# A two-block transformer kernel: TensorE in written order for its first half, head sums on four column groups, VectorE's row steps and weight splits behind each inverse square root

## Chip, core and metric

The kernel runs on one core of one Trainium2 chip, as one launch. The metric is the device time in microseconds (us) from start to end. Engines go by the profile's names: PE (TensorE; PEld is its weight load), DVE (VectorE), ACT (ScalarE), POOL (GpSimd) and SP (SyncE, here a queue of DMAs).

## What is computed

`x` (256 tokens, width 1024, fp32) first goes through two attention layers (layer 0: sliding-window and dilated attention; layer 1: latent attention with rotary keys) and a norm. Then two layers of a second block follow, each with a mixer (differential attention with normed q and k heads, pooling, a convolution, gates) and a mixture of 16,384 experts called PEER. A second stream of 256 context tokens goes through layer 0 of the second block and serves as keys and values in layer 1.

```python
def rms_norm(x, g):
    y = x * lax.rsqrt(jnp.mean(x * x, axis=-1, keepdims=True) + EPS)
    return y * g
def peer_ffn(x, w_q, sub_keys, u_emb, v_emb):   # 8 heads, top 16 each
    s = einsum(x @ w_q, sub_keys); s1, i1 = top_k(s[..., 0, :], 16); s2, i2 = top_k(s[..., 1, :], 16)
    top_s, pos = top_k(s1[:, None] + s2[None, :], 16); eidx = i1 * 128 + i2 at pos
    hid = gelu(einsum('td,thkd->thk', x, u_emb[eidx]))
    return einsum('thk,thkd->td', softmax(top_s) * hid, v_emb[eidx])
```

## The kernel before

Activations lie transposed: 1024 features as 8 chunks of 128 partitions by 256 tokens. A weight matrix comes as chunks of 128 x 1024 numbers (512 KB), loaded by SP's queue for the x stream and by POOL's for the context stream (`WS.load`). To keep precision with the fast matmul type, `WS.split` makes a high part `wa` on ACT (L281) and a low part `wb = wr - wa` on DVE (L282); `mm3` (L409 to L411) then runs three matmuls per 128 rows, 24 per chunk. Chunks marked whole go as native fp32 (`mm1`, L416).

The streams are Python generators that yield a cost after each piece. `par`, `lead` and `along` take turns among them by these costs, so they set the order in which instructions are written. A scheduler with its own clock then reorders the instructions of each engine: a ready one may be put ahead of one that is written earlier. On the chip each engine runs its own list in order.

`rsqrt` (L396 to L403) is a bit trick and three Newton steps, 13 small DVE instructions in a chain. `rms_bcast` squares on ACT (L472), sums over partitions on PE (L474, four 32-column groups), sums per token (L479), calls `rsqrt`, builds a diagonal (`dg`, L498) and broadcasts it with PE (L501). `qkv` (L946) and `attn2` (L1046) sum each head's squares with a matmul that has the 128 x 128 square as its weight and moves 2 columns or 1; after `rsqrt` they transpose the result (`rows_hl`, L905 or L903), split it into `rh` and `rl` (L907, L908) and spread it with `selT` (L966, L967).

PEER for x (`ffn_start`, `topk`, `gbuild`, `peer`): scores and top 16 on DVE; `gbuild` turns the choices into tables G with one-hot products (L1487, L1489 on DVE, L1495 on PE, L1499 on ACT) and stores them; `peer` streams all of U and V, 128 chunks each: `hid(j)` gives chunk j's hidden values, `wgt(j)` multiplies by G (L1551), `vside(j)` adds W times V (L1576 to L1580). The first `npre` hidden chunks run before the main loop, the first `nnat` of them in native fp32; `NPRE` holds both, per layer.

PEER for the context takes each chosen expert's row by indirect DMA (`rows`, L1381): 512 row steps of 128 x 1024 on DVE, half L1392 (dot products), half L1401 (accumulation). They run beside everything from the middle of layer 0's x mixer on, at the rates in `RATE`.

Of the kernel before, what the change touches and what calls it, by code (L numbers as in the profile page):

```python
# [34 lines left out]
NPRE = (16, 20), (20, 28)  # L35
# [16 lines left out]
for _name, _w in (("ident", 128), ("iota", 128), ("perm", 128), ("sel2", 2),  # L52
                  ("ropeC", 256), ("ropeS", 256), ("edge", 64), ("causal", 256),
                  ("iota16", 16), ("starts", 16), ("fold", 32), ("misc", 8)):
    _C[_name] = (_n, _n + _w)
    _n += _w
# [10 lines left out]
def const_tables():  # L67
# [11 lines left out]
    perm = np.zeros((128, 128), np.float32)  # L79
    perm[p ^ 32, p] = 1.0  # L80
    put("perm", perm)
    put("fold", np.concatenate([np.eye(32, dtype=np.float32)] * 4, 0))
    put("sel2", np.stack([p < 64, p >= 64], 1).astype(np.float32))
# [169 lines left out]
class WS:  # L253
# [18 lines left out]
    def split(s, to):  # L272
        nc = s.k.nc
        while s.ns < min(to, s.n):
# [7 lines left out]
            nc.vector.tensor_tensor(b, r, a, op=OP.subtract)  # L282
# [10 lines left out]
class Ker:  # L293
    def __init__(s, nc, tc, es, ai, ao):
# [6 lines left out]
        s.bufs = dict(BUFS)  # L301
        s.cn = 0
# [91 lines left out]
    def rsqrt(s, y, ss, scale, hv, t):  # L394
# [68 lines left out]

    def rms_bcast(s, hch, n):

        nc = s.nc
        st = s.ps("m")
        if n == 8:

            for g in range(0, n, 4):  # L470
                sq = s.pg([128, 4, T], F32, "sq")
                nc.scalar.activation(sq, hch(g, 4), AF.Square)  # L472
                for k in range(4):
# [23 lines left out]
        for tt in range(2):  # L497
            nc.vector.tensor_scalar(dg[:, tt], s.C("ident"), r[:, tt:tt + 1], None, op0=OP.mult)  # L498
        rb = s.ps("m")
# [4 lines left out]
    def rms(s, h, n=8):  # L504
        rbs = s.s1([128, T], "rbs")
        s.nc.vector.tensor_copy(rbs, s.rms_bcast(lambda g, m: h.t[g // 4][:, :], n))
        return rbs

    def norm_hl(s, h, a, b, name, n=8, rbs=None):

        nc = s.nc
        rbs = rbs if rbs is not None else s.rms(h, n)
        o = HL(s, name, n)
        for k in range(n):
# [6 lines left out]
            else:  # L521
                nc.scalar.activation(oh, y, AF.Identity, bias=b(k))
                nc.vector.scalar_tensor_tensor(ol, y, b(k), oh, op0=OP.add, op1=OP.subtract)
        return o

    def norm_f(s, h, a, b, o):

        nc = s.nc
        rbs = s.rms(h)
        for k in range(8):  # L530
            y = s.s1([128, T], "ny")
            nc.vector.scalar_tensor_tensor(y, h.ch(k), a(k), rbs, op0=OP.mult, op1=OP.mult)
            nc.scalar.activation(o.ch(k), y, AF.Identity, bias=b(k))  # L533
        return o
# [88 lines left out]
    def attn_causal(s, scores, bias, init, scale, val, emit):  # L623
# [49 lines left out]
        for i in range(18):  # L673
            if i < 16:
                first(i)
            if 1 <= i < 17:
                second(i - 1)
            if i >= 2 and i % 2 == 1:
                third((i - 3) // 2)
            yield 1.7  # L680
# [12 lines left out]
    def b1(s, x, eng, out):  # L693
# [8 lines left out]
        hn = s.norm_hl(x, lambda k: s.V("norm_w", k), None, "hn")  # L702
        del x
        ws.load(W1)
        yield 1.0
# [1062 lines left out]
```

## Time and profile before

| | us |
|---|---|
| runs of this kernel: median of 3 (lowest, highest) | 3698.21 (3693.96, 3700.71) |
| the profiled execution's own time | 3691.09 |
| its span | 3689.3 |
| PE busy in it | 3258.1 (88%) |
| DVE busy | 2790.7 (76%) |
| ACT busy | 1485.0 (40%) |
| POOL busy | 935.6 (25%) |

The granted TensorE clock is 0.932 of full speed on average. The 16 DMA engines moved 941.10 MB. Busy shares are averages over stages with different limits: by time the trace shows the first block and the context's layer 0 up to 872 us, layer 0's x mixer to 1289, its expert choice to 1410, the tables to 1558, PEER's loop to 2322, layer 1's mixer to 2840, its expert choice and tables to 3010, and its PEER to the end.

### The profile page before, as it was taken

Reading aid. Unit: us, or ns where it says so; the run is one execution under the profiler, and the core shown is the slowest. Engines: PE = TensorE matmul, PEld = TensorE weight load, DVE = VectorE, ACT = ScalarE, POOL = GpSimd, SP = SyncE. Lnnn points to the kernel's source line nnn. Section 1 sums busy time; section 2 is a strip of 40 time slices with the busy share of each in tenths; the row PEclk is TensorE's granted clock in tenths of the full one; section 3 lists DMA queues with packets and bytes.
Section 4 is the critical chain, followed back from the end, with each engine's and each line's share of the span. In section 5 each row is a group of like instructions: output and inputs, shape, how many; then the busy total and the mean of one; then the engine's idle time right before and its main releaser. Section 6 shows DMA issues by size and latency. Waiting matters only on the chain. (4 is left out here: it accounts for less than half of the span.)

```text
span 3689.3 us, 61049 instructions
## 1 busy us (share of the span) xinstructions
PE 3258.1 (88%) x23324; PEld 2966.9 (80%) x23324; DVE 2790.7 (76%) x5722; ACT 1485.0 (40%) x2785; POOL 935.6 (25%) x831
## 2 busy tenths in 40 slices
PE   6989989996799885679999999778998689999999
PEld 5976889766689774668888888767988589999999
DVE  4356585578899889799989999788465978777655
ACT  3444345323355313333443444333353154444443
POOL 2002101212343512365555555232000003111000
PEclk9989999998899897889999999888999899999999
DMA  8536446756688845999999999776525089888764
GB/s 298 160 126 215 146 138 189 274 183 225 238 299 280 321 161 181 344 408 386 384 379 386 379 387 381 248 280 231 158 88 192 12 262 354 307 285 286 263 217 153
DMA packets 315430, 941.10 MB, mean 255 GB/s; under 512 B 29616, under 2 KB 93136, under 8 KB 315136
## 3 DMA queue, kind: packets, MB, share of 16 engines
q1 hardware_dynamic: 130848, 468.77, 35.7%
q0 software_dynamic: 118816, 432.76, 32.3%
q10 hardware_dynamic: 65472, 35.66, 3.2%
q8 instruction: 183, 3.00, 0.3%
q14 instruction: 111, 0.91, 0.1%
HBM read 893.01 MB, written 43.02 MB: 254 GB/s over the span
## 5 line engine op out<-in xcount | busy, mean ns | idle before, releaser
L282 DVE TENSOR_TENSOR wb<-wr,wa 128x1024 fp32r<-128x1024 f32 x846 | 1015.4, 1222 | 321.5 <-ACT wa L281 304.9
L281 ACT CAST wa<-wr 128x1024 fp32r<-128x1024 f32 x846 | 856.3, 1046 | 108.3 <-DMA wr<-in_w 39.0
L409 PE MATMUL pu<-hnh,wa 128*128 128x256 f32 x2000 | 586.0, 293 | 47.9 <-ACT wa L281 45.9
L411 PE MATMUL pu<-hnh,wb 128*128 128x256 f32 x2000 | 583.4, 293 | 17.1 <-DVE wb L282 17.0
L410 PE MATMUL pu<-hnl,wa 128*128 128x256 f32 x2000 | 578.5, 290 | 0.0
L409 PE MATMUL pu<-xh,wa 128*128 128x256 f32 (+1 forms) x1760 | 492.1, 280 | 10.1 <-ACT wa L281 9.6
L1381 POOL DMA_INDIRECT row<-in_pu,ridx x256 | 365.1, 1426 | 520.7 <-DVE wb L282 124.5
L410 PE MATMUL pu<-xl,wa 128*128 128x256 f32 (+1 forms) x1760 | 491.2, 279 | 0.9 <-DVE xl L1538 0.9
L411 PE MATMUL pu<-xh,wb 128*128 128x256 f32 (+1 forms) x1760 | 491.4, 279 | 0.0
L1381 POOL DMA_INDIRECT row<-in_pv,ridx x256 | 354.4, 1384 | 473.5 <-DVE wb L282 133.0
L409 PEld LDWEIGHTS pu<-hnh,wa 128*128 128x128 f32 x2000 | 397.7, 199 | 65.0 <-ACT wa L281 52.0
L411 PEld LDWEIGHTS pu<-hnh,wb 128*128 128x128 f32 x2000 | 395.8, 198 | 32.5 <-DVE wb L282 21.9
L410 PEld LDWEIGHTS pu<-hnl,wa 128*128 128x128 f32 x2000 | 397.4, 199 | 3.9 <-issue 3.5
L409 PEld LDWEIGHTS pu<-xh,wa 128*128 128x128 f32 x1760 | 338.5, 192 | 20.1 <-ACT wa L281 14.5
L410 PEld LDWEIGHTS pu<-xl,wa 128*128 128x128 f32 x1760 | 338.5, 192 | 4.6 <-DVE xl L1538 1.1
L411 PEld LDWEIGHTS pu<-xh,wb 128*128 128x128 f32 x1760 | 338.5, 192 | 1.8 <-issue 0.4
L1401 DVE SCALAR_TENSOR_TENSOR racc<-row,rwg,racc 128x1024 f32<-128x1024 f32 x254 | 325.5, 1282 | 0.4
L416 PE MATMUL pu<-xn,wr 128*128 128x256 f32 (+1 forms) x1344 | 311.9, 389 | 4.7 <-ACT xn L533 4.7
L1392 DVE CUSTOM_DVE_ANT_0 row<-row,xr 128x1024 f32<-128x1024 f32 x256 | 311.2, 1221 | 0.0
L1528 ACT ACTIVATE gel<-pu 128x256 f32<-128x256 f32 (+1 forms) x208 | 77.2, 371 | 577.8 <-PE pu L411 553.0
L416 PEld LDWEIGHTS pu<-xn,wr 128*128 128x128 f32 x1344 | 261.6, 199 | 41.7 <-issue 6.2
L1570 PE MATMUL pm<-W,wa 128*128 128x224 f32 x1024 | 276.1, 275 | 1.6 <-ACT wa L281 1.6
(427 smaller groups left out, 6487.7 us busy)
## 6 DMA issues: line engine op xcount, KB each, us to landing
wr<-in_w SPq DMA_DIRECT2D x288, 512.0 KB
wr<-in_pu SPq DMA_DIRECT2D x256, 512.0 KB
wr<-in_pv SPq DMA_DIRECT2D x256, 512.0 KB
wr<-in_w POOLq DMA_DIRECT2D x130, 512.0 KB
wm<-in_wmod POOLq DMA_DIRECT2D x96, 512.0 KB
G<-gt ACTq DMA_DIRECT2D x60, 512.0 KB
gp<-G SPq DMA_DIRECT2D x32, 512.0 KB
gp<-G SPq DMA_DIRECT2D x32, 448.0 KB
```

The source lines that it names most:

```text
L281: nc.scalar.copy(a, r)
L282: nc.vector.tensor_tensor(b, r, a, op=OP.subtract)
L409: mm(out, ah, bh, start=i == 0, stop=False)
L410: mm(out, ah, bl, start=False, stop=False)
L411: mm(out, al, bh, start=False, stop=i == n - 1)
L416: s.nc.tensor.matmul(out, w[:, k * 128:(k + 1) * 128], x(k), start=k == 0, stop=k == 7)
L1381: nc.gpsimd.indirect_dma_start(out=t, out_offset=None, in_=tab[w], in_offset=bass.IndirectOffsetOnAxis(ap=s.ridx[:, tt, i:i + 1], axis=0))
L1392: v.tensor_tensor_reduce(t, t, xr[tt], 1.0, 0.0, OP.mult, OP.add, hid[:, i:i + 1])
L1401: v.scalar_tensor_tensor(out[tt], t, wg[:, i:i + 1], out[tt], op0=OP.mult, op1=OP.add)
L1528: nc.scalar.activation(g, bank[:, :NT], AF.Gelu_apprx_tanh)
L1570: mm(o, vh[:, c], W[:, 0], start=j == 0 and d % 2 == 0, stop=False, skip_group_check=True)
```

## The change

Seven things change.

1. Everything from the start to the end of layer 0's `ffn_start` is written under `manual_schedule(engines={PE})`: PE's list there is the written order. The other engines are scheduled as before, and PE too from layer 0's PEER loop on.
2. Head sums use the square as the moving side, with a 32-column selection as the weight, one column group per k; ACT copies the result (`gs`), and `by_token` regroups it with two matmuls.
3. `behind()` gives every weight split's DVE half and every context row step an edge behind the last instruction of the latest `rsqrt` written before it. It is an order of issue on DVE, without a wait for data.
4. Norms yield between their parts, so that `par` and `lead` can write another stream's work there. Attention transposes two steps after the scores instead of one.
5. In layer 0, `topk` scores a head one step later and `gbuild` uses its one-hot tiles one step later (`skew`).
6. `EARLY`: in layer 0 the hidden chunks before the loop are written at six times the cost rate beside the rest of `topk`, then beside `gbuild`, 50 against 64.
7. `NPRE` of layer 0 goes from (16, 20) to (20, 24).

```diff
-NPRE = (16, 20), (20, 28)
+NPRE = (20, 24), (20, 28)
+EARLY = 6.0, 50.0
...
             nc.scalar.copy(a, r)
-            nc.vector.tensor_tensor(b, r, a, op=OP.subtract)
+            with s.k.behind():
+                nc.vector.tensor_tensor(b, r, a, op=OP.subtract)
...
-            v.scalar_tensor_tensor(y, t, 1.5, y, op0=OP.add, op1=OP.mult)
+            s.tail = v.scalar_tensor_tensor(y, t, 1.5, y, op0=OP.add, op1=OP.mult)
+    def behind(s):
+        return s.tc.issue_after(s.tail.ins) if s.tail is not None else nullcontext()
...
+    def grouped(s, st):
+        gs = s.s1([128, T], "gs")
+        s.nc.scalar.copy(gs, st[:, :T])
+        return gs
+    def by_token(s, gs, w):
+        n = w.shape[1]
+        o = s.ps("m")[:, :2 * n].rearrange("p (a b) -> p a b", a=2)
+        for tt in range(2):
+            s.nc.tensor.matmul(o[:, tt], gs[:, tt * 128:(tt + 1) * 128], w, start=True, stop=True)
+        return o
...
-                for k in range(4):
-                    f = (0 if off else 16) + 2 * (hf * 4 + k)
-                    for tt in range(2):
-                        mm(bank[:, tt * nc_ + f:tt * nc_ + f + 2], sq[:, k, tt * 128:(tt + 1) * 128], s.C("sel2"),
-                           start=True, stop=True)
+            yield 1.0
+        bank = s.ps("m")
+        for n, (sq, f) in enumerate(sqs):
+            for k in range(4):
+                mm(bank[32 * k:32 * k + 32, :T], s.C("hs")[:, f:f + 32], sq[:, k],
+                   start=n == 0, stop=n == len(sqs) - 1)
+        gs = s.grouped(bank)
+        yield 1.0
+        bank = s.by_token(gs, s.C("hp")[:, :nc_])
...
-            if 1 <= i < 17:
-                second(i - 1)
+            if 2 <= i < 18:
+                second(i - 2)
...
             if w == 0:
-                v.tensor_tensor_reduce(t, t, xr[tt], 1.0, 0.0, OP.mult, OP.add, hid[:, i:i + 1])
+                with s.behind():
+                    v.tensor_tensor_reduce(t, t, xr[tt], 1.0, 0.0, OP.mult, OP.add, hid[:, i:i + 1])
...
-    yield from par(k, (chain(tk, lambda: k.gbuild(rx, G, k.nc.scalar, ntc)), TG), (until(pe), tot), *more)
+    yield from lead(tk, (pre, early))
+    yield from par(k, (k.gbuild(rx, G, k.nc.scalar, ntc), 64.0), (pre, tot))
...
+    with k.tc.manual_schedule(engines={mybir.EngineType.PE}):
```

By the written order, 12 more of the 512 row steps stand before the end of layer 0's x mixer (121 instead of 109), and 48 instead of 58 after PEER's loop.

**PE, layer 0's x mixer, from the head sums to the first spread.** `pm` is a PSUM bank, `sq` the squares, `rr` the inverse square roots, `hnh`/`hnl` and `wa`/`wb` the two parts of activation and weight. Before:

```order
L411 MATMUL pu_9376<-hnh_8327,wb_9151 128x256
L946 MATMUL pm_9177<-ct,sq_9178 128x2 x8
L946 MATMUL pm_9177<-ct,sq_9188 128x2 x8
L946 MATMUL pm_9177<-ct,sq_9198 128x2 x8
L946 MATMUL pm_9177<-ct,sq_9208 128x2 x8
L409 MATMUL pu_9376<-hnh_8327,wa_9150 128x256
L410 MATMUL pu_9376<-hnl_8329,wa_9150 128x256
L411 MATMUL pu_9376<-hnh_8327,wb_9151 128x256
L409 MATMUL pu_9376<-hnh_8327,wa_9150 128x256
L410 MATMUL pu_9376<-hnl_8329,wa_9150 128x256
L411 MATMUL pu_9376<-hnh_8327,wb_9151 128x256
L905 MATMUL pm_9236<-ct,rr_9218 16x128 x2
```

With the change:

```order
L470 MATMUL pu_9112<-wa_9133,hnl_8399 128x512
L988 MATMUL pm_9207<-sq_9196,ct 32x256 x4
L988 MATMUL pm_9207<-sq_9198,ct 32x256 x4
L988 MATMUL pm_9207<-sq_9200,ct 32x256 x4
L988 MATMUL pm_9207<-sq_9202,ct 32x256 x4
L494 MATMUL pm_9226<-ct,gs_9224 128x32 x2
L946 MATMUL pm_9250<-ct,rr_9229 16x128 x2
L1013 MATMUL pm_9299<-rh_9253,selT 128x256
L1014 MATMUL pm_9299<-rl_9254,selT 128x256
```

Before, matmuls of the next branch's weight chunks (L409 to L411; two chunks in all) stood on both sides of the sums; they have moved behind the attention's first scores, and the transposes of `rr` follow the sums by token directly.

**DVE at the same norm.** `row` and `racc` are row steps (ISA is L1392, L1459 with the change), `t` and `k` the rotary steps, `rt` and `rr` the inverse square root's. Before:

```order
L397 TENSOR_SCALAR rr_9218<-rt_1661_9220 128x64
L398 TENSOR_SCALAR rhv_9219<-rt_1661_9220 128x64
L1401 SCALAR_TENSOR_TENSOR racc_9248<-row_9268,rwg,racc_9248 128x1024
L975 TENSOR_TENSOR t_1695_9334<-t_1694_9333,t_1695_9334 128x512
L399 TENSOR_SCALAR rr_9218<-rr_9218 128x64
L1392 ISA row_9281,rhid<-row_9281,xr_8428 128x1024
L1392 ISA rhid 128x1
L1401 SCALAR_TENSOR_TENSOR racc_9248<-row_9300,rwg,racc_9248 128x1024
L401 TENSOR_TENSOR rt_1661_9220<-rr_9218 128x64
L1392 ISA row_9325,rhid<-row_9325,xr_8428 128x1024
L1392 ISA rhid 128x1
L402 TENSOR_TENSOR rt_1661_9220<-rt_1661_9220,rhv_9219 128x64
```

With the change:

```order
L417 TENSOR_TENSOR rt_1679_9231<-rr_9229 128x64
L418 TENSOR_TENSOR rt_1679_9231<-rt_1679_9231,rhv_9230 128x64
L419 SCALAR_TENSOR_TENSOR rr_9229<-rt_1679_9231,rr_9229 128x64
L1469 SCALAR_TENSOR_TENSOR racc_8950<-row_9187,rwg,racc_8950 128x1024
L1459 ISA row_9190,rhid<-row_9190,xr_8158 128x1024
L1459 ISA rhid 128x1
L1459 ISA row_9204,rhid<-row_9204,xr_8158 128x1024
L1459 ISA rhid 128x1
L998 TENSOR_SCALAR sr_9245<-rr_9229 128x32
L1459 ISA row_9257,rhid<-row_9257,xr_8158 128x1024
L1459 ISA rhid 128x1
L949 TENSOR_TENSOR rl_9254<-pm_9250,rh_9253 16x256
```

No row step stands inside the chain any more; four stand between its end (L419) and `rl` (L949), where before one small step stood. Five rotary steps of 128 x 512 are left inside (two before).

**PE at the end of layer 0's expert choice.** `keyT` and `qf` are the key scores, `xn` and `wr` a native hidden chunk, `tt` the transposes of the choice, which `gbuild` waits for. Before:

```order
L416 MATMUL pu_13399<-xn_12692,wr_13393 128x256 x4
L1241 MATMUL pm_13226<-keyT_12761,qf_13224 128x128 x4
L416 MATMUL pu_13497<-xn_12691,wr_13395 128x256 x4
L416 MATMUL pu_13497<-xn_12692,wr_13395 128x256 x4
L416 MATMUL pu_13592<-xn_12691,wr_13397 128x256 x4
L416 MATMUL pu_13592<-xn_12692,wr_13397 128x256 x4
L1241 MATMUL pm_13276<-keyT_12761,qf_13274 128x128 x4
L1344 MATMUL pm_13444<-ct,tt_13445 128x128
L1344 MATMUL pm_13444<-ct,tt_13448 128x128
```

With the change:

```order
L436 MATMUL pu_13508<-xn_12702,wr_13475 128x256 x4
L436 MATMUL pu_13520<-xn_12701,wr_13487 128x256 x4
L436 MATMUL pu_13520<-xn_12702,wr_13487 128x256 x4
L436 MATMUL pu_13540<-xn_12701,wr_13506 128x256 x4
L436 MATMUL pu_13540<-xn_12702,wr_13506 128x256 x4
L1410 MATMUL pm_13558<-ct,tt_13559 128x128
L1410 MATMUL pm_13558<-ct,tt_13562 128x128
L1410 MATMUL pm_13558<-ct,tt_13565 128x128
L1410 MATMUL pm_13571<-ct,tt_13572 128x128
L1410 MATMUL pm_13571<-ct,tt_13575 128x128
L1410 MATMUL pm_13571<-ct,tt_13578 128x128
L436 MATMUL pu_13586<-xn_12701,wr_13518 128x256 x4
L436 MATMUL pu_13586<-xn_12702,wr_13518 128x256 x4
L436 MATMUL pu_13598<-xn_12701,wr_13538 128x256 x4
```

Nine hidden chunks stand between the last scores and the transposes, and two more before the first table; before, three stood in the whole of the expert choice. At the other end, five split hidden chunks stood behind the last table of `gbuild` before; none does with the change.

## Rows read from the trace of the kernel before

**Rows 1.** The page: the span, and the loads of PEER's U chunks (queue, count, KB each).

```profile
span 3689.3 us, 61049 instructions
...
wr<-in_pu SPq DMA_DIRECT2D x256, 512.0 KB
```

**Rows 2.** Windows by stage: us, busy us (instructions) of PE, PEld, DVE, ACT, POOL; clock, DMA share, GB/s.

```profile
46.00:690.00 644.00, 595.35 (x4218) 532.75 (x4218) 377.73 (x841) 289.18 (x532) 84.02 (x158) 0.92 0.52 170
...
872.00:1289.00 417.00, 370.24 (x2730) 347.13 (x2731) 365.03 (x611) 182.59 (x279) 167.06 (x120) 0.93 0.81 282
...
1365.00:1410.00 45.00, 2.35 (x13) 1.55 (x12) 43.84 (x254) 3.93 (x10) 0.94 (x1) 0.56 0.07 24
1410.00:1517.00 107.00, 85.89 (x677) 72.72 (x675) 104.64 (x162) 46.61 (x243) 32.87 (x24) 0.87 0.87 281
1517.00:1558.00 41.00, 22.75 (x162) 21.43 (x163) 21.20 (x28) 14.66 (x46) 13.05 (x11) 0.79 1.00 362
1558.00:2322.00 764.00, 693.88 (x4128) 612.86 (x4126) 707.06 (x945) 309.63 (x484) 423.22 (x293) 0.97 0.99 385
2322.00:2840.00 518.00, 441.16 (x3148) 409.23 (x3147) 361.76 (x644) 211.50 (x325) 76.56 (x69) 0.90 0.56 191
```

**Rows 3.** Waits of PE, 46 to 1289 us: us in total, times, longest.

```profile
PE pm L501 <- DVE dg L498: 25.9, 6, 10.1
PE pm L905 <- DVE rr L403: 12.4, 1, 12.4
```

**Rows 4.** Timeline of PE: the head sums at 952 us; one norm's sums by groups and by token.

```profile
850.94 1.08 PE L474 MATMUL pm<-sq,ones 128*32 128x256 f32 x8 [4.58 <-ACT sq L472]
...
854.08 1.01 PE L479 MATMUL pm<-ct,gs 128*128 128x1 f32 x4 [0.49 <-ACT gs L476]
...
952.00 8.90 PE L946 MATMUL pm<-ct,sq 128*128 128x2 f32 x64
```

**Rows 5.** Count of the sums' matmul records: duration ns min/median/max, first and last start.

```profile
L946 PE MATMUL pm<-ct,sq x224: 169/251/354, 164.6 to 2661.9; 128*128 128x2 f32 x112
...
L1046 PE MATMUL pm<-ones,sq x96: 167/250/353, 266.8 to 2780.0; 128*128 128x1 f32 x96
```

**Rows 6.** Timeline of PE, 170 to 182 us: two matmuls of one form behind a block of head sums.

```profile
175.05 0.63 PE L448 MATMUL pu<-wa,hnh 128*128 128x512 f32 x1
...
180.32 0.39 PE L448 MATMUL pu<-wa,hnh 128*128 128x512 f32 x1
```

**Rows 7.** Timeline of DVE, 955 to 985 us: the inverse square root of layer 0's q and k.

```profile
965.02 0.23 DVE L396 TENSOR_SCALAR rt<-pm 128x64 f32<-128x64 f32 x1
...
967.16 1.29 DVE L1401 SCALAR_TENSOR_TENSOR racc<-row,rwg,racc 128x1024 f32<-128x1024 f32 x1
...
974.51 0.23 DVE L403 SCALAR_TENSOR_TENSOR rr<-rt,rr 128x64 f32<-128x64 f32 x1
...
975.81 0.41 DVE L908 TENSOR_TENSOR rl<-pm,rh 16x256 fp32r<-16x256 f32 x1 [0.86 <-ACT rh L907]
```

**Rows 8.** Timeline of DVE, 2436 to 2462 us: the same of layer 1.

```profile
2438.49 0.22 DVE L396 TENSOR_SCALAR rt<-pm 128x64 f32<-128x64 f32 x1
...
2454.20 0.23 DVE L403 SCALAR_TENSOR_TENSOR rr<-rt,rr 128x64 f32<-128x64 f32 x1
...
2459.54 0.41 DVE L908 TENSOR_TENSOR rl<-pm,rh 16x256 fp32r<-16x256 f32 x1
```

**Rows 9.** Groups of PE, 1365 to 1410 us: busy us, mean ns, idle before and releaser.

```profile
L1344 PE MATMUL pm<-ct,tt 128*128 128x128 f32 x3 | 1.2, 457 | 38.8 <-ACT tt L1343 38.8
```

**Rows 10.** Timeline of PE: one native hidden chunk; all first-table V matmuls, first and last start.

```profile
1526.04 4.26 PE L416 MATMUL pu<-xn,wr 128*128 128x256 f32 x16
...
L1578 PE MATMUL pm<-wa,W x512: 387/395/796, 1560.9 to 2317.0; 128*128 128x512 f32 x171
```

**Rows 11.** Timeline, 200 to 214 us: one attention step, from scores to probabilities.

```profile
200.36 0.70 PE L998 MATMUL pm<-k,q 64*128 64x256 f32 x4
...
204.07 0.49 DVE L1008 SCALAR_TENSOR_TENSOR p<-p,den 128x256 f32<-128x256 f32 x1
```

More of the change, by code (lines that the diff above doesn't have):

```diff
@@ L1 @@
 import math
-from contextlib import ExitStack
+from contextlib import ExitStack, nullcontext
 import numpy as np
@@ L511, in norm_hl @@
         nc = s.nc
-        rbs = rbs if rbs is not None else s.rms(h, n)
+        if rbs is None:
+            rbs = yield from s.rms(h, n)
         o = HL(s, name, n)
@@ L528, in norm_f @@
         nc = s.nc
-        rbs = s.rms(h)
+        rbs = yield from s.rms(h)
         for k in range(8):
@@ L1310, in topk @@
                     yield TY
+        prev = None
+        for h, sb in s.lin(ws, xn, 16):
+            if sb is None:
+                yield 2.6
+                continue
+            qf = s.s2([128, 512], "qf")
+            nc.scalar.copy(qf, sb)
+            if not skew:
+                yield from select(h, qf)
+                continue
+            if prev is not None:
+                yield from select(*prev)
+            prev = h, qf
+        if skew:
+            yield 2.6
+            yield from select(*prev)
+        del prev
         ts = tp[:, 2].rearrange("p h t k -> p (h t) k")
@@ L1400, in rows @@
             else:
-                v.scalar_tensor_tensor(out[tt], t, wg[:, i:i + 1], out[tt], op0=OP.mult, op1=OP.add)
+                with s.behind():
+                    v.scalar_tensor_tensor(out[tt], t, wg[:, i:i + 1], out[tt], op0=OP.mult, op1=OP.add)
             yield 1.0
@@ L1726, in program, with norm_ctx, choose @@
-    drain(along(ffn_start(k, 0, rx, ws, k.G[0], pe, NPRE[0][1] * 3.41), rows, RATE[2]))
+    with k.tc.manual_schedule(engines={mybir.EngineType.PE}):
+        x = [k.h_load(ai["xT"].rearrange("a p k t -> a p (k t)"), sy, "x")]
+        k.setup()
+        ctx0 = ai["ctxT"].rearrange("a p k t -> a p (k t)")
+        hc = [k.h_load(ctx0, sy, "hc")]
+        rc, rx = {}, {}
+        x3, cn, acc = [], [], []
+        b1 = k.b1(x.pop(), sy, x3)
+        md = k.mods(0, gp)
+        rbc = []
+        def norm_ctx():
+            rbc.append((yield from k.rms(hc[0])))
+        drain(par(k, (until(b1), 1.0), (norm_ctx(), 1.0)))
+        drain(until(md))
+        wc = WS(k, ai["w2"][0], gp, whole=WHOLE)
+        def choose():
+            yield from k.topk(0, rc["xn"], wc, gp, rc, rows=True)
+            cn.append(rc.pop("xn"))
+        rows = k.rows(cn, acc)
+        ws = WS(k, ai["w2"][0], sy, whole=WHOLE)
+        ctx = chain(k.mixer(0, 1, ctx0, wc, gp, rc, lambda: [], md, seq=True, h=hc.pop(), rbs=rbc.pop()),
+                    lambda: par(k, (choose(), 69.0), (k.mods(1, gp), 26.0)))
+        xs = chain(b1, lambda: k.mixer(0, 0, k.hd["x"], ws, sy, rx, lambda: [k.kv_load(sy)], seq=SEQ, h=x3.pop()))
+        drain(lead(xs, (chain(ctx, lambda: scaled(rows, RATE[0] / RATE[1])), RATE[0]), (k.setup2(), 0.5)))
+        kp = {}
+        pe = k.peer(0, rx["xn"], k.G[0], sy, sy, *NPRE[0], k.hd["x"], kp)
+        drain(along(ffn_start(k, 0, rx, ws, k.G[0], pe, *EARLY), rows, RATE[2]))
```

197 lines of the change are left out of this document (105 added, 92 removed).

## Prediction

> **What bounds the kernel.** I read the windows by stage first, then the waits of PE, then single places in the timeline. There is no one bound. From 46 to 690 us PE is busy 595.35 of 644 us, and in layer 0's x mixer 370.24 of 417 [rows 2]: PE is the limit there, apart from waits at the norms, six of 25.9 us together for the diagonal and one of 12.4 us for `rr` [rows 3]. The end of the expert choice (1365 to 1410 us) is DVE's: 43.84 of 45 us, while PE has 2.35 us of work and DMA a share of 0.07 [rows 2]. The tables (to 1517) are DVE's too, with 104.64 of 107 us. From 1517 to 1558 neither is full, and DMA has a share of 1.00; PEER's loop stays at 0.99 and 385 GB/s for 764 us [rows 2]. There only bytes count: a load of 512 KB costs 524,288 / 385,000 = 1.36 us. Layer 1's mixer is mixed again, with PE at 441.16 of 518 us [rows 2].
>
> **Term 1: head sums.** A block of 64 records takes 8.90 us, 0.139 us each [rows 4]; there are 224 + 96 such records [rows 5], so 320 x 0.139 = 44.5 us of PE go. What comes: 56 + 24 matmuls in 20 groups of four, 1.08 us a group, seven regroupings of 1.01 us, and seven waits for ACT's copy of 0.49 us [rows 4]: 21.6 + 7.1 + 3.4 = 32.1 us. Those rows follow idle time, and behind a block of old sums a matmul takes 0.63 us against 0.39 us five microseconds later [rows 6], so with PE at its upper clock I halve the first two figures and get 17.8 us. The gain is 12 to 27 us; I take 18, since some blocks lie under other work.
>
> Here the rows speak against a rule. The Trainium skill (TensorEngine Tiling (Array Packing), Performance Considerations) says that a matmul has about 60 cycles of overhead, so one of a single column costs no more than one of 60. As an estimate from that page, 320 records of 60 cycles at 2.4 GHz are 8 us, and the new form would lose 10 to 24 us instead. The measured 0.139 us is over five times as much, so the trace disagrees and the row decides.
>
> **Term 2: the inverse square root.** In layer 0's mixer the chain lasts from 965.02 to 974.74 us, 9.7 us, for 13 small steps of 0.23 us or less, which overlap; row steps of 1.29 us stand among them [rows 7]. In layer 1 it lasts from 2438.49 to 2454.43, 15.9 us [rows 8]. Free of strangers it would be at most 13 x 0.23 = 3.0 us, so 20 us seem to be there. But the order shows where the row steps go: four of them behind the chain's end, ahead of `rl`, 4 x 1.29 = 5.2 us, and five rotary steps stay inside, estimated at half a row step, 0.65 us. So layer 0's place goes from 9.7 us plus 1.07 us to `rl` [rows 7] to about 6.3 + 5.5: one microsecond worse. Layer 1's goes from 15.9 plus 5.1 us [rows 8] to 6.3 + 9.0 (five row steps and two splits, each counted as a row step): 6 better. At norms of the full width the order puts three row steps ahead of the diagonal, 3.9 us, at four exposed places of the x stream; in two of these about as much other work stood inside the chain before, which leaves 2 x 3.9 = 8 us. Together +3, and one or two row steps more ahead of the copy of the broadcast. Weight splits held back cost nothing while PE has two split chunks ahead (48 matmuls). I take +5 us; bounds -20 (the row steps don't stand in the way on the chip) and +15.
>
> **Term 3: expert choice and tables of layer 0.** PE waits 38.8 us for the transposes [rows 9]. A native hidden chunk takes 4.26 us at a mixed clock [rows 10], so nine of them, 38 us, fit beside 45 us of DVE. They need loads where DMA is nearly idle: eleven chunks instead of three before the first table are eight loads, 8 x 1.36 = 11 us off the DMA-bound stretch. Five split chunks no longer trail the tables; V started at 1560.9 us [rows 10], and the loop has to wait for the stores of G in either case. Four chunks go native instead of split, which costs PE time and spares DVE four splits; both hide under DMA. The bounds are 0 and 41 us (the whole stretch from 1517 to 1558 [rows 2]). I take -16: 11 for the bytes and 5 for the emptier queues.
>
> **Term 4: PE in written order.** It helps where a norm of one stream now has 24 matmuls of another between its parts: of the 25.9 us of waits for the diagonal [rows 3] I count 12. It costs where the scheduler had pulled work forward: two chunks at layer 0's mixer, 48 x 0.11 = 5 us, and the regrouping followed directly by the transposes of `rr` in the context's `qkv`, where PE went on at once before [rows 6]. Attention should not suffer: from scores to probabilities takes 204.56 - 200.36 = 4.2 us [rows 11], and with the transposes two steps back some 6 us of PE's work lie between. I take -6 us, between -35 and +60.
>
> **Term 5: row steps.** Twelve more, with their gathers on POOL's queue, lie before the end of layer 0's mixer, where DMA has a share of 0.81 [rows 2], and ten fewer in layer 1's. Ten steps of 1.29 us are 13 us of DVE in a stage where DVE is busy 361.76 of 518 us [rows 2], so most hide. I take -3 (-12 to +5).
>
> **The sum.** -18 + 5 - 16 - 6 - 3 = -38 us. The profiled execution took 3691.1 us (span 3689.3 us [rows 1] and 1.8 us around it), 7.1 us under the median of the runs, 3698.2; 3653 there is **3660 us** against the median.
>
> **The rivals.**
> *PE's waits add up (slower).* With the written order nothing ready can jump a wait. For it speaks that the old lists pulled work ahead at almost every norm; against it, the 4.2 us of an attention step. There are 64 such steps in the first half and layer 0; a stall of 1 us at each and of 4.6 us at four norms without other work is 82 us, so -38 - (-6) + 82 = +50: 3748 us. It decides from about 0.7 us a step.
> *More than the parts.* If the norms and steps were laid so that half of PE's idle time from 46 to 690 and 872 to 1289 us (48.7 + 46.8 us [rows 2]) is filled, 48 us come instead of 6: 3618 us; at a higher clock 3600. The clock of 0.92 and 0.93 there speaks for it; the same idle time, already small after the old scheduling, against.
> *It does nothing.* The row steps only change places, the head sums lay under ACT, and DMA takes back what the tables save, so 3698 us. The share of 0.99 in the loop [rows 2] speaks for the last; the idle DMA of 0.07 before it against.
>
> **How the numbers follow.** My sum 0.55, with its own range of 3630 to 3690; more than the parts 0.17; nothing 0.08; slower 0.20. A measurement of this kernel tells 0.2% (7.4 us) from no change. A part of the sum's chance, 0.02, lies on slow ends of terms 2 and 4 together. So faster 0.70, same 0.08, slower 0.22. The range reaches from 3595 to 3716: it leaves out the deepest part of the second case and most of the slower one.
>
> **What would show it.** Right: head-sum blocks of 1 to 4 us instead of 8.90; nine native chunks under the choice's end with PE busy over 30 of those 45 us; V's first matmul some 15 us earlier within its stage; the loop unchanged at 0.99; four row steps between chain and `rl`. Wrong: PE's idle time from 46 to 690 us over 60 us, waits for transposes `pm<-ct,p` in every attention step, or a gap at `dg` longer than before without a gain elsewhere. If layer 0's mixer loses over 20 us, the second rival was the case.

## The result, and the profile after

The changed kernel takes **3631.26 us** (median of 4 runs, 3628.18 to 3634.04), the kernel before beside it 3697.47 us: a ratio of 0.9821, 95% interval 0.9804 to 0.9838, so 66 us less (60 to 72). I had forecast 3660 us, 38 less. The profiled execution lies on the median (3631.59 us, of which the span is 3629.5).

To see where the time went I cut both traces at the same events on PE: 46 us, the last diagonal ahead of layer 0's x mixer, the diagonal of that mixer's second norm, the first and the last V matmul of layer 0, the diagonal of layer 1's second norm, and layer 1's first V matmul. The stretches in us, for the two kernels and for all that follow below:

| kernel | front | x mixer | choice, tables | loop 0 | mixer 1 | choice 1 | loop 1 |
|---|---|---|---|---|---|---|---|
| before | 817.9 | 425.4 | 271.7 | 758.3 | 514.7 | 236.6 | 618.9 |
| after | 775.8 | 431.3 | 266.1 | 756.0 | 494.0 | 241.4 | 618.9 |
| e1 no `behind` | 779.0 | 440.8 | 267.9 | 759.6 | 490.1 | 238.3 | 618.9 |
| e2 old sums | 789.5 | 438.8 | 267.2 | 757.3 | 498.4 | 240.9 | 619.0 |
| e3 scheduled | 789.1 | 429.8 | 273.5 | 756.5 | 495.6 | 235.5 | 618.9 |
| e4 old start | 772.6 | 436.0 | 281.7 | 752.8 | 492.3 | 237.2 | 618.9 |
| e5 before + `behind` | 824.4 | 427.0 | 273.6 | 761.0 | 525.7 | 236.0 | 618.9 |
| e6 one step | 809.5 | 440.6 | 267.5 | 755.7 | 509.3 | 237.2 | 618.9 |
| e7 all written | 780.0 | 434.8 | 266.6 | 801.8 | 502.4 | 233.0 | 622.7 |
| e8 before + written | 829.1 | 441.7 | 275.4 | 761.7 | 514.2 | 240.4 | 618.9 |
| e9 before + two steps | 805.2 | 425.0 | 272.6 | 756.8 | 503.2 | 237.4 | 618.9 |
| e10 rows held | 759.5 | 438.5 | 265.2 | 756.6 | 508.9 | 237.7 | 618.9 |
| e11 more rows | 774.0 | 434.5 | 269.2 | 765.8 | 458.1 | 234.2 | 618.9 |
| e12 neither | 798.8 | 437.4 | 271.5 | 756.3 | 509.6 | 237.1 | 618.9 |

With the change 42 us fall in the front, 6 in choice and tables, 2 in the loop and 21 in layer 1's mixer; layer 0's x mixer is 6 us longer, and so, by 5, is layer 1's choice. That makes 60 us of the 66: the profiled execution of the kernel before lay 6 us under its median. Each stretch is read from one execution, and whole runs of one kernel scatter by 6 us and more, so a few us of difference in this table may be chance.

Windows by stage of after, then those of the kernel before for the three stretches that moved most (columns as in [rows 2]):

```profile
46.00:821.80 775.80, 707.06 (x5126) 613.75 (x5124) 506.56 (x1527) 325.00 (x614) 128.64 (x223) 0.94 0.59 200
821.80:1253.20 431.40, 361.65 (x2695) 336.97 (x2694) 374.00 (x622) 186.73 (x286) 161.88 (x124) 0.90 0.79 278
1341.00:1383.00 42.00, 40.79 (x184) 35.14 (x184) 39.78 (x203) 9.18 (x24) 2.30 (x2) 0.97 0.16 51
1519.30:2275.30 756.00, 683.57 (x4010) 601.70 (x4011) 696.70 (x927) 302.46 (x471) 424.93 (x290) 0.96 0.99 387
2275.30:2769.30 494.00, 420.35 (x3100) 387.05 (x3098) 348.74 (x628) 208.41 (x321) 75.41 (x60) 0.91 0.56 185
```

```profile
46.00:863.90 817.90, 741.43 (x5114) 638.12 (x5114) 496.91 (x1499) 322.15 (x608) 115.31 (x212) 0.92 0.53 180
863.90:1289.30 425.40, 372.18 (x2738) 348.37 (x2737) 371.56 (x625) 187.11 (x288) 168.13 (x122) 0.92 0.81 282
2319.20:2833.90 514.70, 438.42 (x3153) 407.31 (x3150) 360.88 (x642) 208.93 (x319) 78.48 (x70) 0.90 0.55 188
```

The first columns of the front say something that I had not looked for: PE's idle time there (window less busy time) only goes from 76.5 to 68.7 us, but its busy time from 741.4 to 707.1. The work of the front got faster; the waits hardly fewer. In layer 0's x mixer it is the other way round: 10.5 us less busy time and 16.5 us more idle time. In the choice's end PE works 40.79 of 42 us (2.35 of 45 before, [rows 2]).

Single places of after: head sums of layer 0's q and k on PE; the end of the inverse square root behind them on DVE; and PE's groups at the end of the choice.

```profile
908.49 0.64 PE L988 MATMUL pm<-sq,ct 128*32 128x256 f32 x8 [2.38 <-ACT sq L983]
...
910.38 2.03 PE L988 MATMUL pm<-sq,ct 128*32 128x256 f32 x16 [0.30 <-issue]
912.90 1.06 PE L494 MATMUL pm<-ct,gs 128*128 128x32 f32 x4 [0.49 <-ACT gs L486]
922.73 0.60 PE L946 MATMUL pm<-ct,rr 128*16 128x128 f32 x2 [8.77 <-DVE rr L419]
```

```profile
916.78 0.23 DVE L412 TENSOR_SCALAR rt<-pm 128x64 f32<-128x64 f32 x1
...
922.45 0.23 DVE L419 SCALAR_TENSOR_TENSOR rr<-rt,rr 128x64 f32<-128x64 f32 x1
922.59 1.28 DVE L1469 SCALAR_TENSOR_TENSOR racc<-row,rwg,racc 128x1024 f32<-128x1024 f32 x1
923.79 1.22 DVE L1459 CUSTOM_DVE_ANT_0 row<-row,xr 128x1024 f32<-128x1024 f32 x1
...
926.17 1.22 DVE L1459 CUSTOM_DVE_ANT_0 row<-row,xr 128x1024 f32<-128x1024 f32 x1
...
927.31 0.41 DVE L949 TENSOR_TENSOR rl<-pm,rh 16x256 fp32r<-16x256 f32 x1
```

```profile
L436 PE MATMUL pu<-xn,wr 128*128 128x256 f32 x176 | 39.7, 388 | 0.0
L1410 PE MATMUL pm<-ct,tt 128*128 128x128 f32 x6 | 1.5, 318 | 1.2 <-ACT tt L1409 1.1
```

The block of [rows 4], 8.90 us, is now 5.5 us with its gaps, 908.49 to 913.96. The chain lasts 5.9 us instead of 9.7 [rows 7], four row steps stand between its end and `rl`, which starts 10.5 us after the chain's start instead of 10.8. The wait for the transposes, 38.8 us in [rows 9], is 1.2 us.

### The profile page after: what moved, and what is told of

The parts are those of the page before. It is cut to its first block, busy times and chain, and to the rows that moved or that the text cites. A ratio compares the mean times of both kernels' runs of the same rounds, so it can differ in the third digit from the quotient of the medians.

```text
span 3629.5 us, 60668 instructions
## 1 busy us (share of the span) xinstructions
PE 3205.7 (88%) x23160; PEld 2911.8 (80%) x23160; DVE 2780.5 (77%) x5718; ACT 1484.5 (41%) x2788; POOL 936.3 (26%) x831
## 5 line engine op out<-in xcount | busy, mean ns | idle before, releaser
L297 DVE TENSOR_TENSOR wb<-wr,wa 128x1024 fp32r<-128x1024 f32 x842 | 1010.3, 1222 | 289.8 <-ACT wa L295 267.2
L1447 POOL DMA_INDIRECT row<-in_pu,ridx x256 | 357.4, 1396 | 516.6 <-DVE wb L297 92.3
L429 PE MATMUL pu<-xh,wa 128*128 128x256 f32 (+1 forms) x1728 | 484.1, 280 | 0.9 <-ACT xh L1618 0.9
L430 PE MATMUL pu<-xl,wa 128*128 128x256 f32 (+1 forms) x1728 | 483.3, 280 | 1.5 <-DVE xl L1619 1.5
L1447 POOL DMA_INDIRECT row<-in_pv,ridx x256 | 362.6, 1417 | 466.4 <-DVE wb L297 113.3
L431 PE MATMUL pu<-xh,wb 128*128 128x256 f32 (+1 forms) x1728 | 482.8, 280 | 0.0
L429 PEld LDWEIGHTS pu<-xh,wa 128*128 128x128 f32 x1728 | 333.3, 193 | 10.3 <-ACT wa L295 4.3
L436 PE MATMUL pu<-xn,wr 128*128 128x256 f32 (+1 forms) x1408 | 325.8, 390 | 4.4 <-ACT xn L573 4.4
L1459 DVE CUSTOM_DVE_ANT_0 row<-row,xr 128x1024 f32<-128x1024 f32 x256 | 311.0, 1221 | 5.6 <-issue 5.2
L436 PEld LDWEIGHTS pu<-xn,wr 128*128 128x128 f32 x1408 | 276.3, 200 | 44.9 <-issue 7.5
```

The source lines that it names most:

```text
L429: mm(out, ah, bh, start=i == 0, stop=False)
L430: mm(out, ah, bl, start=False, stop=False)
L431: mm(out, al, bh, start=False, stop=i == n - 1)
L436: s.nc.tensor.matmul(out, w[:, k * 128:(k + 1) * 128], x(k), start=k == 0, stop=k == 7)
L1447: nc.gpsimd.indirect_dma_start(out=t, out_offset=None, in_=tab[w], in_offset=bass.IndirectOffsetOnAxis(ap=s.ridx[:, tt, i:i + 1], axis=0))
L1459: v.tensor_tensor_reduce(t, t, xr[tt], 1.0, 0.0, OP.mult, OP.add, hid[:, i:i + 1])
```

## The experiments

Gains and losses below are the differences of ratios times 3697 us. One ratio is known to about 6 us either way, a difference of two to about 9.

**e1: the changed kernel without the wait**

```diff
     def behind(s):
-        return s.tc.issue_after(s.tail.ins) if s.tail is not None else nullcontext()
+        return nullcontext()
```

> The changed kernel (3631 us, 66 us under the one before) with the wait of row steps and weight splits behind the inverse square root taken out, everything else kept; PE's written order up to the end of layer 0's start is then the same. Theory A (the ordering helps where a chain is bare, above all in layer 1's mixer, which fell from 515 to 495 us, by 20 us, of which the head sums explain about 11): 8 to 15 us are lost, 3639 to 3646 us, and the chain of layer 1's q and k is long again (over 12 us from its first to its last step). Theory B (my prediction's term 2: the wait only puts the row steps behind the chain's end, at a loss of 5 us): 3626 us. Theory C (it is neutral, because DVE does the same work a few us later): 3631, within 4 us.

Measured: 3644.11 us, ratio 0.9868 (0.9849 to 0.9886), 17 us lost. Theory A in size, but not in place: layer 1's chain is long again, 27.9 us, and its mixer is 4 us *shorter* than with the wait. The largest piece of the loss is layer 0's x mixer, 431.3 to 440.8. PE's longest waits there for `rr` and `rl`, first of e1 and then of after:

```profile
PE pm L946 <- DVE rr L419: 20.3, 1, 20.3
PE pm L944 <- DVE rr L419: 14.0, 1, 14.0
```

```profile
PE pm L946 <- DVE rr L419: 8.8, 1, 8.8
...
PE pm L1110 <- DVE rl L949: 5.3, 1, 5.3
```

The chain of 13 steps takes 18.5 us in e1, with five row operations of each of the two kinds inside, where it took 9.7 in the kernel before. PE, in written order, takes nothing else meanwhile.

**e2: the changed kernel with the old head sums**

```diff
-                mm(bank[32 * k:32 * k + 32, :T], s.C("hs")[:, f:f + 32], sq[:, k],
-                   start=n == 0, stop=n == len(sqs) - 1)
+                for tt in range(2):
+                    mm(bank[:, tt * nc_ + f:tt * nc_ + f + 2], sq[:, k, tt * 128:(tt + 1) * 128], s.C("sel2"),
+                       start=True, stop=True)
```

(and the same for the attention's output, without regrouping.)

> The changed kernel with the head sums of q, k and the attention's output as 320 single records again (one matmul per head pair and token half, straight into one column or two, no regrouping, no copy), the rest kept. Theory A (term 1 as summed, 18 us): 3649 us, some 8 us of it before 830 us, and the rest in the two x mixers. Theory B (the records also hold PE at its lower clock behind them, so matmuls that follow are slower too): over 3660 us, with a granted clock in the first 600 us below 0.95 instead of 0.97. Theory C (the blocks lie under waits that remain, so little comes back): under 3638 us.

Measured: 3650.03 us, 0.9873 (0.9854 to 0.9891), 19 us lost: theory A. By place it is 14 us in the front, 7 or 8 in the x mixer and 4 in layer 1's mixer (e2's profiled execution is 9 us above its median, so the places add up to more than 19). The clock to 600 us is 0.95 (0.97 after), so B's effect is there, but small.

**e3: the changed kernel with PE scheduled**

```diff
-    with k.tc.manual_schedule(engines={mybir.EngineType.PE}):
+    with nullcontext():
```

> The changed kernel with PE's order chosen by the scheduler everywhere again, instead of as written up to the end of layer 0's start; the yields at the norms, the attention's third step back and all else stay. The stretch up to the start of layer 0's x mixer fell from 872 to 828 us with the change, by 43 us: 36 us of that in PE's busy time, 7 in its idle time. Theory A (written order fills PE at norms, and a PE that does not stop keeps the upper clock): 3660 to 3670 us, start of the x mixer back near 860 us, granted clock up to 600 us down from 0.97 to about 0.92. Theory B (the new places of the yields and the third step back do that, whoever orders): within 8 us of 3631. Theory C (written order costs where something ready cannot jump a wait, as the x mixer of layer 0 with 425 instead of 418 us hints): 3615 to 3625 us.

Measured: 3647.18 us, 0.9876 (0.9859 to 0.9892), 20 us lost, 13 of them in the front and 7 at the tables. The size lies below A's, and A's reason fails: the clock to 600 us stays at 0.97, and PE's idle time in the front is smaller than after. It is busy time that grew, from 707.1 to 727.5 us (46 to 835.1 us). The group that grew most are the matmuls of `mods`, which computes the second block's modulation vectors. In the front (busy us, mean ns, idle before), of after, of e3 and of the kernel before:

```profile
L615 PE MATMUL pm<-wm,cs 128*32 128x512 f32 x320 | 50.6, 625 | 0.0
```

```profile
L615 PE MATMUL pm<-wm,cs 128*32 128x512 f32 x320 | 66.9, 603 | 0.0
```

```profile
L574 PE MATMUL pm<-wm,cs 128*32 128x512 f32 x320 | 60.7, 607 | 0.0
```

One place of each in PE's timeline, again after first:

```profile
300.19 1.06 PE L615 MATMUL pm<-wm,cs 128*32 128x512 f32 x8
```

```profile
303.33 1.05 PE L615 MATMUL pm<-wm,cs 128*32 128x512 f32 x4
```

Eight of these records take 1.06 us in one order, four take 1.05 in the other. A matmul of native fp32 that is no transpose leaves two records here (the 16 of the head sums in the list of the written order are 32 in the trace), so these are four matmuls and two. They go to four column groups: the eight records start as two sets of four, the four as two sets of two, and a set of two takes as long as one of four. By the starts of all 320 records, the written order runs 64 sets of four and 32 of two, the scheduler's 32 of four and 90 of two, with a few odd ones. That is 16 of the 20.4 us of busy time; against the kernel before (60.7 us) the change wins 10 us by it. The 7 us at the tables were not followed up.

**e4: the changed kernel with the old start of the expert stage**

```diff
-NPRE = (20, 24), (20, 28)
+NPRE = (16, 20), (20, 28)
...
-        drain(along(ffn_start(k, 0, rx, ws, k.G[0], pe, *EARLY), rows, RATE[2]))
+        drain(along(ffn_start(k, 0, rx, ws, k.G[0], pe, None, NPRE[0][1] * 3.41), rows, RATE[2]))
```

> The changed kernel with the start of layer 0's expert stage as before: hidden chunks spread over choice and tables, no group of choices or tables held back by one step, 16 native chunks of 20 ahead instead of 20 of 24. Theory A (term 3: bytes moved into the idle stretch of DMA, 16 us): 3647 us, V's first matmul again some 260 us behind the end of the x mixer instead of 265 less 12 us. Theory B (the stages show only 8 us: 271 us from the x mixer's end to V before, 265 after, and 2 us in the loop): 3639 us. Theory C (the loop waits for the last store of G in either case and gives all back): 3631, within 4 us.

Measured: 3641.04 us, 0.9855 (0.9836 to 0.9875), 13 us lost, between A and B. Choice and tables take 281.7 instead of 266.1 us; the loop gives 3 back. The windows of e4 from the tables' end to V, and of the loop:

```profile
1501.00:1536.30 35.30, 24.97 (x154) 23.54 (x153) 17.12 (x22) 13.03 (x32) 12.79 (x12) 0.84 0.97 337
1536.30:2289.10 752.80, 684.42 (x4106) 605.28 (x4107) 703.10 (x936) 307.26 (x479) 413.86 (x291) 0.98 1.00 389
```

The first is 35.3 us with 25 us of trailing hidden chunks; in after it is 17.3 us with almost nothing, the wait for V's first split:

```profile
1519.27 2.08 PE L1659 MATMUL pm<-wa,W 128*128 128x512 f32 x4 [17.14 <-ACT wa L295]
```

Of the 15.6 us only 5.6 are a gain against the kernel before, whose choice and tables take 271.7 us: with the change's other parts the old start does worse than it did before.

**e5: the kernel before, with the wait alone**

```diff
-            nc.vector.tensor_tensor(b, r, a, op=OP.subtract)
+            with s.k.behind():
+                nc.vector.tensor_tensor(b, r, a, op=OP.subtract)
```

(and around the two row operations, with `tail` set as in the change.)

> The kernel before with one addition: row steps and weight splits wait for the last step of the latest inverse square root. Taking that wait out of the changed kernel cost 15 to 17 us, with the chain of q and k in the x mixer 18.5 us long (5.9 with the wait), although in the kernel before it was only 9.7 us long. Theory A (the wait mends what the other parts of the change bring about, twelve more row steps in that mixer and a PE that cannot jump; alone it does what term 2 said): +5 us, between -4 and +9, so 3695 to 3707 us. Theory B (the wait is worth the same in either kernel): about 3680 us.

Measured: 3714.65 us, 1.0056 (1.0041 to 1.0071), 21 us *slower*. Neither theory: A has the sign and not the size. It costs 6.5 us in the front, 3 in the loop and 11 in layer 1's mixer, whose window shows as much idle time as before (76 us), but 449.53 us of PE instead of 438.42, at a clock of 0.88 instead of 0.90:

```profile
2332.10:2857.80 525.70, 449.53 (x3151) 417.01 (x3150) 361.79 (x642) 208.29 (x319) 80.83 (x70) 0.88 0.56 184
```

**e6: the changed kernel with attention one step back, as before**

```diff
-        for i in range(19):
+        for i in range(18):
...
-            if 2 <= i < 18:
-                second(i - 2)
-            if i >= 3:
-                third(i - 3)
-            yield 2.85
+            if 1 <= i < 17:
+                second(i - 1)
+            if i >= 2:
+                third(i - 2)
+            yield 3.0
```

(and the other attention likewise.)

> The changed kernel with both attention loops as before: the transposes one step behind the scores and the products one more, 18 steps instead of 19; the rest kept. Layer 1's mixer, where PE is still ordered by the scheduler, went from 515 to 494 us, and none of the four parts taken out so far gives more than 4 us of that back. Theory A (the longer distance between scores and transposes is what layer 1 gained from, and with written order it is needed): layer 1's mixer back at 505 us or more, and with written order waits of PE for the probabilities of about 1 us in each of 80 steps, in all 3660 to 3710 us. Theory B (4.2 us from scores to probabilities are covered by the other work in between anyway): within 8 us of 3631, and layer 1's gain comes from its ten fewer row steps.

Measured: 3688.04 us, 0.9989 (0.9981 to 0.9998): 62 us lost, nearly the whole gain. Theory A. It is 33.7 us in the front, 9.3 in the x mixer and 15.3 in layer 1's mixer. PE's waits at the transposes of the probabilities `p` from 46 us to the x mixer's end, in e6 and then in after:

```profile
PE pm L1062 <- DVE p L1055: 25.5, 10, 5.7
...
PE pm L697 <- DVE p L690: 16.6, 6, 5.1
```

```profile
PE pm L1062 <- DVE nb L1049: 5.9, 4, 3.3
...
PE pm L697 <- DVE p L690: 5.3, 3, 1.9
```

Sixteen stalls, not the one at each step that A named, and more than their own time is lost. The front of e6:

```profile
46.00:855.50 809.50, 722.28 (x5125) 624.33 (x5124) 509.58 (x1524) 326.41 (x614) 129.48 (x224) 0.92 0.57 192
```

With the same matmuls as after, 33.7 us come back: 18.5 of idle time and 15.2 of busy time, the latter at a granted clock of 0.92 instead of 0.94 (2.5 us of it are smaller sets in `mods`, 53.1 us there). From 190 to 330 us, where eleven of the stalls lie, the clock is 0.80 in e6 and 0.91 in after:

```profile
190.00:330.00 140.00, 114.08 (x684) 88.51 (x688) 83.66 (x304) 65.08 (x190) 14.28 (x27) 0.80 0.41 139
```

```profile
190.00:330.00 140.00, 130.37 (x889) 99.28 (x890) 100.72 (x368) 78.35 (x225) 22.42 (x43) 0.91 0.53 182
```

One stall of e6 and what follows it: the matmuls behind it start 0.21 us apart, those 1.5 us later 0.12.

```profile
191.96 0.66 PE L1062 MATMUL pm<-ct,p 128*128 128x128 f32 x2 [3.22 <-DVE p L1055]
...
196.97 0.41 PE L429 MATMUL pu<-hnh,wa 128*128 128x256 f32 x1
197.18 0.41 PE L430 MATMUL pu<-hnl,wa 128*128 128x256 f32 x1
...
198.42 0.28 PE L429 MATMUL pu<-hnh,wa 128*128 128x256 f32 x1
198.54 0.28 PE L430 MATMUL pu<-hnl,wa 128*128 128x256 f32 x1
```

**e7: PE in written order to the end of the program**

```diff
-    rx.clear()
-    drain(along(pe, rows, RATE[3]))
...
+        rx.clear()
+        drain(along(pe, rows, RATE[3]))
...
```

> The changed kernel with PE in written order to the end of the program, the loops and layer 1 too, instead of only up to the end of layer 0's start. Theory A (written order gains where the code yields at a norm; layer 1 has four such places without a second stream, so nothing stands there to fill them, and the tables of layer 1 lose the scheduler's freedom): 3628 to 3645 us. Theory B (it gains in layer 1 as it did up to 830 us): below 3620 us. Theory C (the loops deadlock their own flow, U and V chunks waiting for each other's weight splits): over 3660 us.

Measured: 3687.59 us, 0.9983 (0.9972 to 0.9993): theory C in size (no deadlock, a slow flow). The loop takes 801.8 instead of 756.0 us, with 28.5 us of waits for `wb` at V's second matmul (3.8 after):

```profile
PE pm L1660 <- DVE wb L297: 28.5, 32, 1.8
```

```profile
1527.40:2329.20 801.80, 712.71 (x4034) 621.71 (x4035) 700.26 (x929) 302.23 (x472) 388.32 (x292) 0.93 0.95 365
```

Of the 45.8 us, 16.7 are idle time of PE and 29.1 busy time, at a clock of 0.93 instead of 0.96.

The mixer of layer 1 gains nothing, 502.4 against 494.0 us.

**e8: the kernel before, with written order alone**

```diff
+    with k.tc.manual_schedule(engines={mybir.EngineType.PE}):
...
-    drain(along(ffn_start(k, 0, rx, ws, k.G[0], pe, NPRE[0][1] * 3.41), rows, RATE[2]))
+        drain(along(ffn_start(k, 0, rx, ws, k.G[0], pe, NPRE[0][1] * 3.41), rows, RATE[2]))
```

> The kernel before with one addition: PE in written order up to the end of layer 0's start; no new yields, so a norm's sums, its diagonal's and the broadcast follow each other directly, and attention has its old steps. Theory A (the order pays only together with the yields, which put another stream's matmuls between a norm's parts): slower than before, by the waits at some eleven norms of 3 to 10 us and at the attention steps, 3730 to 3790 us. Theory B (the order itself pays): 3675 to 3685 us, as taking it out of the changed kernel cost 18 us.

Measured: 3727.21 us, 1.0091 (1.0067 to 1.0114), 34 us slower: theory A's sign, at the edge of its size. The same edit gains 20 us in one kernel and loses 34 in another.

**e9: the kernel before, with two steps alone** (the reverse of e6's diff)

> The kernel before with one addition: in both attention loops the transposes stand two steps behind the scores and the products one behind them, 19 steps, as in the changed kernel. Undoing this alone in the changed kernel cost about 60 us: 34 us before 830 us, 9 in layer 0's x mixer, 15 in layer 1's. Theory A (a step is too short for the 4.2 us from scores to probabilities in any order, and the waits also hold PE at its lower clock): the three attention stretches of b1 shrink from 59, 48 and 111 us to about 52, 32 and 94, and the kernel gains 25 to 45 us: 3650 to 3670 us. Theory B (only a PE in written order needs the distance; the scheduler pulls other matmuls between anyway): within 8 us of 3693.

Measured: 3666.79 us, 0.9940 (0.9926 to 0.9953), 22 us gained, just under A. It is 12.7 us in the front and 11.5 in layer 1's mixer: the longer distance pays where the scheduler orders PE, too. The front's 12.7 us are 10.3 of idle time and only 2.4 of busy time, so the busy time that came on top in e6 is not a fixed price of a stall:

```profile
46.00:851.20 805.20, 739.01 (x5115) 635.40 (x5115) 495.40 (x1499) 321.63 (x608) 114.84 (x212) 0.93 0.52 182
```

**e10: the changed kernel with nine row steps held back**

```diff
-        rows = k.rows(cn, acc)
+        rows = hold(k.rows(cn, acc), 9)
...
+def hold(g, n):
+    for _ in range(n):
+        yield 1.0
+    yield from g
```

> The changed kernel with the row steps held back by nine, so that as many remain for layer 1's mixer as in the kernel before (53 operations of 128x1024 behind layer 1's first norm instead of 44). Theory A (the row steps gate the context's norm and with it keys and values of layer 1: its diagonal came 23 us earlier after the loop with nine fewer, about 2.4 us a step): layer 1's mixer takes 494 + 20 = 514 us again, the first half gains a few us of DVE and DMA back, in all 3640 to 3652 us. Theory B (my term 5: most of a step hides, so -3 us for all): within 5 us of 3631.

Measured: 3633.06 us, 0.9837 (0.9820 to 0.9854): 6 us lost, which the intervals can't tell from nothing. By stage it is two large pieces: layer 1's mixer 15 us longer, and the front 16 us shorter (x mixer 7 longer). By DVE's records, 13 row steps of after run ahead of the x mixer, from 789 us on, and none of e10's; in the kernel before the first starts at 878 us, 14 us into that mixer and not in its middle. So nine row steps are 15 us of layer 1's path, and ahead of the x mixer they cost as much as they save.

**e11: the changed kernel with more row steps in the loop**

```diff
-RATE = 2.0, 0.32, 0.25, 0.45, 0.3, 2.0
+RATE = 2.0, 0.32, 0.25, 0.5, 0.3, 2.0
```

> The changed kernel with 0.50 instead of 0.45 row steps a unit of the loop of layer 0, so that 34 more of them lie in that loop and 10 instead of 44 remain behind layer 1's first norm. Each brings 512 KB into a stretch where DMA has a share of 0.99, 1.36 us a step, 46 us in all, and takes about 2.3 us off the path of layer 1's mixer as long as the steps gate it. Theory A (they gate it to the end): the loop takes 800 us instead of 756, the mixer 420 to 440 instead of 494, in all 3600 to 3620 us. Theory B (after the first ten or so something else gates, such as the x stream's own norm and weights): the mixer stops near 470, the loop still loses 46, in all 3650 us.

Measured: **3602.89 us**, 0.9763 (0.9750 to 0.9776), 21 us less than the changed kernel by the ratios (28 between the medians, which were measured at different times). The windows of its loop and of layer 1's mixer:

```profile
1523.70:2289.60 765.90, 686.81 (x4010) 604.24 (x4011) 734.78 (x975) 302.74 (x472) 453.40 (x323) 0.96 1.01 404
2289.60:2747.70 458.10, 413.23 (x3100) 383.61 (x3098) 310.71 (x580) 207.99 (x320) 20.29 (x27) 0.93 0.49 162
```

The total is theory A's, by another account: 32 more row steps lie in the loop (323 of DVE's records, 291 in after); the mixer falls by 36 us, 1.1 us a step and not 2.3, and the loop pays 10 us, not the 46 that both theories gave it.

**e12: the changed kernel with PE scheduled and attention one step back** (the diffs of e3 and e6 together)

> The changed kernel with both edits at once: PE ordered by the scheduler everywhere, and both attention loops one step back as before. Measured so far against the kernel before: -66 us with written order and two steps, -46 with scheduled order and two steps, -4 with written order and one step. Theory A (written order needs the distance: with one step it stalls at the transposes, with two it doesn't): written order costs 15 us or more at one step, so this kernel is at -20 to -35 us, a ratio of 0.990 to 0.995. Theory B (written order gains its 20 us through the yields at the norms, whatever the distance): this kernel is 16 to 20 us above the one with written order and one step, +12 to +16 us, a ratio of 1.003 to 1.005. Theory C (the two simply add nothing to each other beyond noise): about the same as written order with one step, 0.999.

Measured: 3673.43 us, 0.9946 (0.9933 to 0.9960), 20 us under the kernel before: theory A. The four cases, all with the change's other parts, in us against the kernel before:

| | one step back | two steps back |
|---|---|---|
| PE scheduled | -20 (e12) | -46 (e3) |
| PE in written order | -4 (e6) | -66 (after) |

Written order costs 16 us at one step and gains 20 at two. What it trades at one step stands in PE's waits from 46 us to the x mixer's end, of e12 and then of e6: 58 us instead of 32 for the two halves of the weights, 12 instead of 42 for the probabilities (whose rows of e6 stand above).

```profile
PE pu L429 <- ACT wa L295: 32.2, 12, 6.4
PE pu L431 <- DVE wb L297: 26.1, 14, 8.0
...
PE pm L697 <- DVE p L690: 7.2, 3, 3.1
PE pm L1062 <- DVE p L1055: 4.9, 2, 3.7
```

```profile
PE pu L429 <- ACT wa L295: 17.9, 6, 6.4
...
PE pu L431 <- DVE wb L297: 14.2, 11, 3.6
```

## Why the prediction was right, and where its sum was not

The direction and the range hold. The sum of -38 is 28 us short, and the table of the four cases says where. My terms 1, 2, 3 and 5 made -32; all that the change holds beside the order and the distance is -20 (e12). Two steps back are -26 more, where I had nothing. The order then is -20, where I had -6.

The parts do not add. Taken out of the changed kernel one at a time, the wait, the head sums, the early start and the earlier row steps lose 17, 19, 13 and 6 us (e1, e2, e4, e10), 55 in all, and e12, which has them all, gains 20. With e5's loss of 21 in place of the 17 the four would make -17, close to e12. So the wait seems to pay only beside the written order or the longer distance; no run here separates the two.

**Term 1, head sums: right.** -18 forecast, 19 by e2, beside the change's other parts. The rule of the Trainium skill (TensorEngine Tiling (Array Packing), Performance Considerations) that I set against the rows, some 60 cycles of overhead for a small matmul, would by my estimate from that page have made it a loss of 10 to 24 us; e2 does not bear it out.

**Term 2, inverse square root: the places right, the account wrong.** Four row steps behind the chain and 10.5 us from its start to `rl` is what I had read from the order (11.8 estimated), and at layer 0's second norm three row operations stand ahead of the diagonal, as counted (1248.5 to 1252.0 us). In layer 1 the chain is 5.9 us long and `rl` starts 15.2 us after its start (15.9 and 21.0 before), 6 us better, as worked out. The failing step is the base: I set these against the chain of the *old* kernel, 9.7 us. With the change's other parts and no wait it would be 18.5 us, and PE waits 20.3 us for it (e1). So the wait, which I put at +5, gains 17 here, while alone it costs 21 (e5), more than my upper bound of +15 for the term. Why layer 1's mixer pays 11 us of that through slower matmuls was not isolated.

**Term 3, choice and tables: right in size beside the other parts.** -16 forecast; 13 by e4, but by the stretches only 8 against the kernel before (6 in choice and tables, 2 in the loop). Eleven native chunks (176 records), two more than I had counted, cover the choice's end, V starts 17 us behind the last matmul of the tables instead of 30, and by e4 the loop gives 3 us back.

**Term 4, written order: the step that failed.** I wrote that attention should not suffer, since 4.2 us from scores to probabilities fit under some 6 us of PE's work; with two steps back that is so. But I took this as no cost and not as a gain, as if one step had been enough before. It wasn't: PE already waited for `p` in the attention of the first block (`b1`); the row stood in the waits of the kernel before, from 46 to 1289 us, and I passed over it:

```profile
PE pm L656 <- DVE p L649: 10.4, 4, 3.9
```

Two steps alone gain 22 us (e9), and order and distance together 46 (e12 to after), beyond my bound of -35 for the term. The rest of the term, fewer waits for diagonals, is true in small: 21.0 us in four waits from 46 to 1300 us instead of 25.9 [rows 3]. What I had not seen at all is that a written order keeps matmuls of four column groups together: 16 us of busy time against e3, 10 against the kernel before.

**Term 5, row steps: right in sum, by luck in its parts.** -3 forecast, 6 with an error of 9 by e10; but that is 15 us of layer 1's path, where I had "most hide", against 9 us lost ahead of it (16 in the front less 7 in the x mixer).

**The rivals.** *PE's waits add up* is what happens to this order at one step: e6 and e8. It needed fewer stalls than I thought, sixteen, with busy time at a lower clock on top. *More than the parts* lay nearer with 3618 us than my sum, but not by its mechanism: idle time fell by 8 us in the front, rose by 16.5 in the x mixer, and was nowhere halved. *It does nothing* had the row steps nearly right, but the head sums were worth 19 us (e2), and the loop took nothing back of what the tables saved (758.3 to 756.0 us).

## What to carry to other kernels

Before an engine's order is fixed, lengthen the distance between a producer and its consumer by a step: at one step the fixed order cost 16 us, at two it gained 20. Cost each part of a change against the kernel that has the other parts, not against the old one; the wait behind the inverse square root is worth +21 us alone and -17 beside the change's other parts. And where a change has moved the bound, look at what gates the next stage: a single number for the row steps was worth another 21 us.

## What the runs showed of the hardware that I had not expected

The records of four matmuls on four column groups of 32 start some 7 ns apart, and their second records 0.45 us later; if another instruction order lets only two of them meet, these two take the same time (1.05 against 1.06 us, e3). The Trainium skill (TensorEngine Tiling (Array Packing), Tiling Modes) says that tiles work independently and in parallel, which the sets of four show, and that a change of the mode drains the engine, which no run here measures by itself.

A DMA share of 0.99 was not a limit of bytes. From after to e11 the loop's rate rose from 387 to 404 GB/s at a share of 0.99 and 1.01; 32 more row steps (16.8 MB, 44 us at 385 GB/s) took 10 us. My sentence that "only bytes count" in that loop is refuted, and what does bound it stays open.
